# Second feed-forward layer: each quarter of w_ff2 is loaded in the product that first uses it

## The chip, the cores and the metric

The kernel runs on one core of one Trainium2 chip. The metric is the time of one execution in microseconds (us) on the device. Lower is better.

## The reference

One block of a hybrid encoder: 1024 tokens and 16 leading meta tokens of width 1024, everything in float32.

```python
h = h + hybrid_mixer(rmsnorm(h, norm_mix), ...)        # pooling mixer and gated linear attention
h = h + squared_relu_mlp(rmsnorm(h, norm_ffn), w_ff1, w_ff2)
return rmsnorm(h, norm_final)[:, N_META:]

def squared_relu_mlp(u, w_ff1, w_ff2):
    hdn = jnp.square(jax.nn.relu(jnp.einsum('bld,df->blf', u, w_ff1)))   # 1024 -> 4096
    return jnp.einsum('blf,fd->bld', hdn, w_ff2)                         # 4096 -> 1024
```

The change is in the last product, `hdn` by `w_ff2`, and in the loads for it.

## The kernel before

**Arithmetic.** A float32 operand is split in two parts, `hi` (rounded by ScalarE to the matmul's type) and `lo` (the rest, by VectorE); `split` (line 259) issues both, lines 264 and 265. A product is then three matmuls, hi by hi, lo by hi and hi by lo (`mm3`, lines 246 to 248).

**Two layers, in seven products each.** Both feed-forward layers use a Strassen-Winograd scheme: both operands are cut in 2 by 2 quarters, and seven products of sums of quarters take the place of eight. In the first layer, `Quarters.run` makes the hidden values, `ff_result` (line 1490) forms the sums of hidden quarters that the second layer needs, and `keep` stores them in DRAM, one array `hf_dram` for each of the seven (line 1488). There are 16 items (`NPAIR`) of 128 hidden rows in each quarter.

The second layer goes over this table, product by product. A row has the sum of hidden quarters, the sum of quarters of `w_ff2`, and where the result is added (row half, column half, sign):

```python
    FF2 = [
        (S2, "11", ((1, 0, 1), (1, 1, -1))),
        (A22, "21-11", ((0, 0, 1), (1, 0, 1))),
        (S1, "11+22", ((0, 0, 1), (1, 1, 1))),
        (A11, "12-22", ((0, 1, 1), (1, 1, 1))),
        (S6, "11+12", ((1, 1, 1),)),
        (S5, "22", ((0, 0, -1), (0, 1, 1))),
        (S7, "21+22", ((0, 0, 1),)),
    ]
```

So quarter "11" is first used in product 0, "21" in product 1, "22" in product 2 and "12" in product 3.

**One step.** A step is one item `i` of one product `m`. `ff2_raw` (line 1537) issues its loads: `ff2_load` brings the 256 KB of hidden values, called `a` here (the trace names the tile `raw`), into one of four slots, `S["a2"]`; `ff2_weight` brings 256 KB of a quarter of `w_ff2` into its place in `S["w2"]`, where it stays to the end (line 1535). `ff2_operands` (line 1550) forms the sum or difference of two quarters on VectorE, `bt`, in one of two buffers (line 1556), and splits `a` and the weight, each into one of seven slots (`w1h`/`w1l` and `fxh`/`fxl` in the trace). `ff2` (line 1582) then runs 12 matmuls, three into each of four PSUM banks (a bank for each 128 tokens). After the last item of a product the four banks are added to `c` by `add` (lines 1597 and 1599), one addition for each following step.

`c` holds the residual, 8 rows of 512 KB. Row `t` is 128 tokens; rows 0 to 3 are row half 0, rows 4 to 7 row half 1. It is loaded from `h_dram` (line 1547). Products add into rows 4 to 7 after product 0, and into rows 0 to 7 after product 1.

**How far ahead.** `ahead(items, n)` (line 268) runs a generator n items ahead of its user: the loads are issued two items ahead of the operands, the operands two items ahead of the matmuls. A load of `a` has to wait until its slot was split four items before; a split has to wait until TensorE has read the slot it goes to.

**Order.** The order of the instructions on TensorE is that of the program (`manual_schedule`). On the other engines, and on SyncE, which issues all these loads and stores, it is fixed when the program is built, by a scheduler that takes the program's order as its priority and can put an instruction that it holds ready ahead of an earlier one that it doesn't. At run time each engine goes through its order one by one, and one that waits holds up all behind it on its engine.

**Memory.** `ff2_open` (line 1516) lays `w2` and `c` over places of the first layer. "11" lies over operands of the first layer, "21" partly over others that are read to its last product, and `c` over `h`, out of which the last hidden sums are stored. The first load into each has to wait until the last reader of what lay there is done.

In the last product, whose result ends the kernel, the final norm and the stores follow (`finish_row`).

Of the kernel before, what the change touches and what calls it, by code (L numbers as in the profile page):

```python
# [105 lines left out]
def kernel(  # L106
# [1420 lines left out]
    def ff2_load(m, i):  # L1527
        at = S["a2"][(m * NPAIR + i) % len(S["a2"])]
        nc.sync.dma_start(at, hf_of[FF2[m][0]][i])
        return at  # L1530

    def ff2_weight(q, i):
        j, k = int(q[0]) - 1, int(q[1]) - 1
        f = 2 * i + j
        nc.sync.dma_start(S["w2"][q][:, i], w_ff2[f * P : (f + 1) * P, k * HALF : (k + 1) * HALF])

    def ff2_raw():
        for m in range(7):
            for i in range(NPAIR):
                if m == 0:  # L1540
                    ff2_weight("11", i)
                a = ff2_load(m, i)
                if m < 3:
                    ff2_weight(("21", "22", "12")[m], i)
                if m == 0 and i % 2:
                    t = i // 2
                    nc.sync.dma_start(S["c"][:, t], h_dram[t])
                yield m, i, a

    def ff2_operands():  # L1550
        for m, i, a in ahead(ff2_raw(), 2):
            q = FF2[m][1]
            w = S["w2"][q[:2]][:, i]
            if len(q) > 2:
                bt = S["bt"][:, i % 2]
                dve.tensor_tensor(bt, w, S["w2"][q[3:]][:, i], ALU.add if q[2] == "+" else ALU.subtract)  # L1556
                w = bt
            yield m, i, split(a), split(w)
# [140 lines left out]
```

## Time and profile before

| | |
|---|---|
| time, median of 3 | 1243.65 us (1243.61 to 1248.66) |
| the profiled execution's own time | 1241.63 us |
| its span, first to last instruction | 1239.6 us |
| mean granted TensorE clock | 0.996 |
| TensorE matmul busy | 1206.1 us, 97% |
| VectorE busy | 850.9 us, 69% |
| ScalarE busy | 618.8 us, 50% |
| moved by DMA | 173.84 MB, mean 140 GB/s |

Product 0 begins at 923.6 us of the span, and the last matmul starts at 1231.6. The first load into `w2` is issued at 912.2, the last at 1006.7; the eight loads of `c` at 933.2 to 958.6.

In the lines of the profile PE is TensorE's matmul, PEld its weight load, DVE VectorE, ACT ScalarE, and SPq the issuing of DMAs on SyncE. A line of the timeline has the start and duration in us, engine, line and operation, output and inputs, their shapes, and in brackets the idle time of the engine before it and what ended it. A matmul's duration reaches over the start of the next, so the rate is read from the starts.

### The profile page before, as it was taken

Reading aid. Unit: us, or ns where it says so; the run is one execution under the profiler, and the core shown is the slowest. Engines: PE = TensorE matmul, PEld = TensorE weight load, DVE = VectorE, ACT = ScalarE, POOL = GpSimd, SP = SyncE. Lnnn points to the kernel's source line nnn. Section 1 sums busy time; section 2 is a strip of 40 time slices with the busy share of each in tenths; the row PEclk is TensorE's granted clock in tenths of the full one; section 3 lists DMA queues with packets and bytes.
Section 4 is the critical chain, followed back from the end, with each engine's and each line's share of the span. In section 5 each row is a group of like instructions: output and inputs, shape, how many; then the busy total and the mean of one; then the engine's idle time right before and its main releaser. Section 6 shows DMA issues by size and latency. Waiting matters only on the chain.

```text
span 1239.6 us, 18265 instructions
## 1 busy us (share of the span) xinstructions
PE 1206.1 (97%) x6816; PEld 1003.1 (81%) x6816; DVE 850.9 (69%) x1388; ACT 618.8 (50%) x1099; POOL 66.6 (5%) x74
## 2 busy tenths in 40 slices
PE   7999999999999999899999999999999999999997
PEld 6878888988887778688878888888887788888886
DVE  6896676654556676634896676776774877887686
ACT  6667567322446663412654454555553444444554
POOL 2100000001101015400000000000000000000000
PEclk9999999999999999899999999999999999999999
DMA  8033326146102247831244444444569863333432
GB/s 250 2 110 104 110 86 193 53 155 219 36 19 78 69 133 234 282 109 51 98 125 159 156 153 143 162 156 134 176 216 374 289 235 102 94 99 98 162 98 89
DMA packets 142680, 173.84 MB, mean 140 GB/s; under 512 B 10968, under 2 KB 82416, under 8 KB 142592
## 3 DMA queue, kind: packets, MB, share of 16 engines
q1 hardware_dynamic: 142592, 172.68, 43.3%
q8 instruction: 53, 0.87, 0.3%
q14 instruction: 35, 0.29, 0.1%
HBM read 119.17 MB, written 53.48 MB: 139 GB/s over the span
## 4 chain that ended last, share of the span: by engine, by line
PE 85%; DVE 8%; ACT 3%; DMA 2%; issue 2%; SPq 0%; DVEq 0%; ACTq 0%
PE b_mm L246 10%; PE b_mm L247 10%; PE b_mm L248 10%; PE b_ms L247 9%; PE b_ms L246 9%; PE b_ms L248 9%; PE b_x L248 8%; PE b_x L246 8%; PE b_x L247 8%; PE b_sc L1147 1%; PE b_ms L550 1%; PE b_mx L246 1%; PE b_m L1249 1%; PE b_mx L247 1%; PE b_mx L248 1%
## 5 line engine op out<-in xcount | busy, mean ns | idle before, releaser
L246 PE MATMUL b_mm<-th,w1h 128*128 128x512 f32 (+1 forms) x312 | 117.6, 377 | 1.9 <-DVE c L761 1.1
L247 PE MATMUL b_mm<-tl,w1h 128*128 128x512 f32 (+1 forms) x312 | 116.0, 372 | 0.6 <-DVE tl L1407 0.6
L248 PE MATMUL b_mm<-th,w1l 128*128 128x512 f32 (+1 forms) x312 | 115.8, 371 | 0.0
L246 PE MATMUL b_x<-th,w1h 128*128 128x512 f32 (+1 forms) x240 | 90.8, 378 | 0.0
L247 PE MATMUL b_x<-tl,w1h 128*128 128x512 f32 (+1 forms) x240 | 90.6, 378 | 0.0
L248 PE MATMUL b_x<-th,w1l 128*128 128x512 f32 (+1 forms) x240 | 90.3, 376 | 0.0
L264 ACT ACTIVATE w1h<-raw 128x512 fp32r<-128x512 f32 x96 | 59.6, 621 | 36.8 <-PE b_x L247 14.1
L265 DVE TENSOR_TENSOR w1l<-raw,w1h 128x512 fp32r<-128x512 f32 x96 | 65.6, 684 | 12.9 <-ACT w1h L264 12.9
L246 PEld LDWEIGHTS b_mm<-th,w1h 128*128 128x128 f32 x312 | 58.6, 188 | 13.7 <-issue 1.8
L264 ACT ACTIVATE w1h<-fs 128x512 fp32r<-128x512 f32 x72 | 45.4, 631 | 45.8 <-PE b_ms L247 31.5
L247 PEld LDWEIGHTS b_mm<-tl,w1h 128*128 128x128 f32 x312 | 58.6, 188 | 10.6 <-DVE tl L1407 0.9
L248 PEld LDWEIGHTS b_mm<-th,w1l 128*128 128x128 f32 x312 | 58.6, 188 | 10.3
L264 ACT ACTIVATE w1h<-bt 128x512 fp32r<-128x512 f32 x44 | 27.8, 632 | 67.7 <-issue 59.6
L265 DVE TENSOR_TENSOR w1l<-fs,w1h 128x512 fp32r<-128x512 f32 x72 | 49.3, 685 | 14.7 <-ACT w1h L264 14.6
L1556 DVE TENSOR_TENSOR bt<-w,w 128x512 f32<-128x512 f32 x80 | 54.6, 683 | 1.0 <-DMA w<-in_w_ff_dram 1.0
L248 PEld LDWEIGHTS b_x<-th,w1l 128*128 128x128 f32 x240 | 45.1, 188 | 8.4
L246 PEld LDWEIGHTS b_x<-th,w1h 128*128 128x128 f32 x240 | 45.0, 188 | 8.5
L247 PEld LDWEIGHTS b_x<-tl,w1h 128*128 128x128 f32 x240 | 45.1, 188 | 8.3
L264 ACT ACTIVATE fxh<-bt 128x512 fp32r<-128x512 f32 x36 | 22.8, 632 | 55.4 <-issue 48.1
L246 PE MATMUL b_ms<-wo,w1h 128*128 128x512 f32 x128 | 49.8, 389 | 0.0
L247 PE MATMUL b_ms<-wo,w1h 128*128 128x512 f32 x128 | 49.8, 389 | 0.0
L248 PE MATMUL b_ms<-wo,w1l 128*128 128x512 f32 x128 | 49.8, 389 | 0.0
(446 smaller groups left out, 3365.2 us busy)
## 6 DMA issues: line engine op xcount, KB each, us to landing
hf_dram<-h SPq DMA_DIRECT2D x112, 256.0 KB, 2.1
raw<-hf_dram SPq DMA_DIRECT2D x112, 256.0 KB, 2.7
w<-in_w_ff_dram SPq DMA_DIRECT2D x64, 256.0 KB, 4.9
raw<-in_w_in_dram SPq DMA_DIRECT2D x24, 512.0 KB, 4.9
raw<-in_w_ff_dram SPq DMA_DIRECT2D x16, 512.0 KB, 4.1
rawx<-in_w_ff_dram SPq DMA_DIRECT2D x16, 512.0 KB, 4.1
xs<-in_x_dram SPq DMA_DIRECT2D x8, 512.0 KB, 4.7
rawx<-in_w_in_dram SPq DMA_DIRECT2D x8, 512.0 KB, 4.7
```

The costliest lines, as they stand in the source:

```text
L246: pe.matmul(ps, ah, bh, start=first and i == 0, stop=False, skip_group_check=more)
L247: pe.matmul(ps, ah, bl, start=False, stop=False, skip_group_check=more)
L248: pe.matmul(ps, al, bh, start=False, stop=last and i == n - 1, skip_group_check=more)
L264: act.activation(hi, a, ACT.Copy)
L265: dve.tensor_tensor(lo, a, f32(hi), ALU.subtract)
L550: pe.transpose(b[j][:, i], u[:, (4 * j + i) * P : (4 * j + i + 1) * P], ident)
L1147: pe.matmul(b[to, e, j], kk[r, s], qq[r, s], start=True, stop=True, tile_position=(e * CH, u * CH))
L1249: pe.matmul(o[part(u), e, j], scc[part(u), e, j], v[part(u), j, e], start=j == 0, stop=False, tile_position=(u * CH, u * CH), skip_group_c ...
L1556: dve.tensor_tensor(bt, w, S["w2"][q[3:]][:, i], ALU.add if q[2] == "+" else ALU.subtract)
```

## The change

The loads change places in the program, and nothing else. In product 0 only "11" is loaded beside `a`; "21" is loaded in product 1, "22" in product 2, "12" in product 3, each item's weight behind the same item's `a`. Before, "21" came in product 0, "22" in product 1 and "12" in product 2. The rows of `c` came with every second item of product 0, rows 0 to 7 in order; now rows 4 to 7 come with every fourth item of product 0, and rows 0 to 3 with every fourth item of product 1.

```diff
                 if m == 0:
                     ff2_weight("11", i)
                 a = ff2_load(m, i)
-                if m < 3:
-                    ff2_weight(("21", "22", "12")[m], i)
-                if m == 0 and i % 2:
-                    t = i // 2
+                if 0 < m < 4:
+                    ff2_weight(("21", "22", "12")[m - 1], i)
+                if m < 2 and i % 4 == 3:
+                    t = 4 * (1 - m) + i // 4
                     nc.sync.dma_start(S["c"][:, t], h_dram[t])
                 yield m, i, a
```

## The prediction

> **What bounds the kernel now.** I read the page first, then the busy time by stretches, then the matmuls one by one where a stretch isn't full, then the chain of waits back from each gap. On the page (engine busy times, and the chain that ended last by engine):
>
> ```profile
> PE 1206.1 (97%) x6816; PEld 1003.1 (81%) x6816; DVE 850.9 (69%) x1388; ACT 618.8 (50%) x1099; POOL 66.6 (5%) x74
> PE 85%; DVE 8%; ACT 3%; DMA 2%; issue 2%; SPq 0%; DVEq 0%; ACTq 0%
> ```
>
> TensorE bounds it, and the change leaves every matmul as it is. So it can win only what TensorE idles in the second layer, and lose only by new idling there. The stretches of that layer (product 0 with the start of product 1; the rest of product 1; the rest; columns: length, busy time and count by engine, clock, DMA share, GB/s):
>
> ```profile
> 923.00:971.00 48.00, 45.78 (x199) 36.45 (x197) 26.61 (x44) 19.27 (x33) 0.00 (x0) 1.00 0.98 354
> 971.00:1015.00 44.00, 44.00 (x195) 36.42 (x195) 36.22 (x59) 19.75 (x36) 0.00 (x0) 1.00 0.84 277
> 1015.00:1226.00 211.00, 211.00 (x933) 174.74 (x932) 164.63 (x279) 96.45 (x178) 0.00 (x0) 1.00 0.34 102
> ```
>
> Only the first has idle time, 2.22 us, at a DMA share of 0.98; from 971 on TensorE is full. The matmuls around the gaps (start, duration, line, tiles):
>
> ```profile
> 939.73 0.39 PE L248 MATMUL b_ms<-fxh,w1l 128*128 128x512 f32 x1
> 941.25 0.50 PE L246 MATMUL b_x<-fxh 128*128 128x512 f32 x1 [1.14 <-ACT fxh L264]
> ...
> 942.55 0.39 PE L247 MATMUL b_x<-fxl,fxh 128*128 128x512 f32 x1
> ...
> 960.70 0.39 PE L246 MATMUL b_x<-fxh 128*128 128x512 f32 x1
> ...
> 963.19 0.39 PE L248 MATMUL b_ms<-fxh,fxl 128*128 128x512 f32 x1
> 964.59 0.50 PE L246 MATMUL b_x<-w1h 128*128 128x512 f32 x1 [1.01 <-ACT w1h L264]
> ...
> 965.97 0.40 PE L247 MATMUL b_x<-w1l,w1h 128*128 128x512 f32 x1
> ```
>
> From 960.70 to 963.19 twelve matmuls start, so one takes 2.49/11 = 0.226 us, and a step of 12 takes 2.72 us. The first gap: 939.73 to 942.55 is 5 starts, 2.82 us instead of 1.13, so 1.69 us are lost with the slow restart behind it. The second: 963.19 to 965.97 is 5 starts, 2.78 instead of 1.13, so 1.65 us. Together 3.3 us, 0.27% of the kernel. This is the most the change can take from the profiled run.
>
> **Where the two gaps come from.** The first, by the chain of waits in order of time:
>
> ```profile
> 928.45 4.65 DMA hf_dram<-h
> 933.23 0.33 SPq L1547
> 933.60 0.43 SPq L1547
> 934.08 1.40 SPq L1547
> 935.52 5.02 DMA raw<-hf_dram
> 940.57 0.64 ACT fxh L264
> ```
>
> The sync queue held the first three loads of `c` (line 1547). `c` lies where `h` lay, so the first of them waited until the last store out of `h` had landed at 933.1. Behind them stood the load of item 6 of product 0 (935.52), which then took 5.02 us. Its slot in `a2` had been free since VectorE ended the split of item 2 at 923.6, 11.9 us earlier:
>
> ```profile
> 922.93 0.68 DVE L265 TENSOR_TENSOR fxl<-raw,fxh 128x512 fp32r<-128x512 f32 x1
> ```
>
> The second gap is one of order on ScalarE:
>
> ```profile
> 960.70 0.63 ACT L264 ACTIVATE w1h<-w 128x512 fp32r<-128x512 f32 x1 [2.08 <-DMA w<-in_w_ff_dram]
> 963.39 0.63 ACT L264 ACTIVATE fxh<-bt 128x512 fp32r<-128x512 f32 x1 [2.06 <-PE b_ms L247]
> 963.92 0.61 ACT L264 ACTIVATE w1h<-raw 128x512 fp32r<-128x512 f32 x1
> ```
>
> At 963.39 ScalarE split `bt`, which only product 1 needs, and had waited for a slot that TensorE gave back. Behind it in its fixed order stood the split of the `raw` that product 0 needed next (963.92), and TensorE waited for that one. `bt` could be so early because the quarter "21" was already there in product 0.
>
> **What the change removes and moves.** Sizes and landings, the last line from a stretch where the loads of `a` are alone and the line before it from 940 to 970:
>
> ```profile
> w<-in_w_ff_dram SPq DMA_DIRECT2D x64, 256.0 KB, 4.9
> c<-h_dram SPq DMA_DIRECT2D x8, 512.0 KB, 6.6
> ...
> raw<-hf_dram SPq DMA_DIRECT2D x11, 256.0 KB, 6.0
> ...
> raw<-hf_dram SPq DMA_DIRECT2D x34, 256.0 KB, 2.7
> ```
>
> No load is added or dropped: 64 of `w2`, 8 of `c`, 112 of `a`. In program order product 0 now asks for 48 loads of 256 KB and 8 of 512 KB, 16.8 MB in 16 x 2.72 = 43.5 us, 386 GB/s. After the change it asks for 32 and 4, 10.5 MB, 241 GB/s. Product 1 goes from 8.4 MB (193 GB/s) to 10.5 (241), product 2 stays at 193, product 3 goes from 4.2 MB (96) to 8.4 (193). All of these lie under the 354 GB/s that the first stretch moved. The cost in bytes is nil, and the peak is cut by over a third.
>
> *First gap.* Item 6 now comes in the program behind one load of `c` (with item 3) instead of three, and behind no load of "21". The sync queue before it:
>
> ```profile
> 912.23 2.33 SPq L1535 DMA_DIRECT2D w<-in_w_ff_dram  x5
> ...
> 918.36 1.88 SPq L1535 DMA_DIRECT2D w<-in_w_ff_dram  x4
> ...
> 925.25 1.63 SPq L1535 DMA_DIRECT2D w<-in_w_ff_dram  x3
> ...
> 928.83 1.84 SPq L1535 DMA_DIRECT2D w<-in_w_ff_dram  x3
> ...
> 1005.73 1.38 SPq L1535 DMA_DIRECT2D w<-in_w_ff_dram  x3
> ```
>
> If the `c` load still stands ahead of it and waits until 933.1, item 6 issues two loads of `c` earlier, 935.52 - 0.43 - 1.40 = 933.7, and lands between 2.7 and 6.0 us later, 936.4 to 939.7. With the split of 0.64 TensorE could start at 937.0 to 940.4, where it needs it at 939.73 + 0.23 = 939.96. The loss is 0 to 0.4 us plus its slow restart, instead of 1.69. If it goes ahead of `c`, the loss is nil. I take nil, since the load beside it falls.
>
> *Second gap.* "21" now comes behind all of "11", so the first `bt` of product 1 is ready later, and items 14 and 15 land sooner. The split of `raw` should come first. Bounds 0 to 1.65 us of gain; I take 1.65, because both things that made the wrong order are weakened.
>
> *What is late next: the weights of products 1 to 3.* Each load now stands right behind the `a` load of its own item, and that waits for a slot. The `a` load of item 0 of product 3 (the 49th) and the `bt` of the same item (the 33rd), when all runs smoothly:
>
> ```profile
> 1040.72 0.32 SPq L1529 DMA_DIRECT2D raw<-hf_dram  x1
> ...
> 1048.77 0.68 DVE L1556 TENSOR_TENSOR bt<-w,w 128x512 f32<-128x512 f32 x1
> ...
> DMA to landing us min/median/max: 3.0/4.9/7.2
> ```
>
> A weight issued behind that load, at 1041.05, has 1048.77 - 1041.05 = 7.7 us until VectorE wants it. The third line is the landing of all 64 weight loads, in the crowded stretch: median 4.9, worst 7.2. So even strictly just in time it is hidden, by 0.5 us at worst. If that cover went, VectorE would wait at `bt`, with the two `lo` subtractions and the additions into `c` queued behind it, and TensorE behind those. It may not come to that: at 1005.73 the last weight of product 2 is issued while TensorE is still in product 1, so the queue runs ahead of the program when `a` loads wait for slots. Rows 0 to 3 of `c` are used first after product 1, rows 4 to 7 after product 0: each comes with the product before. Cost 0.
>
> Sum: 3.3 us off. The profiled run took 1241.63 us for a span of 1239.6 (2.03 outside), so 1238.3 for that run. It was 2.02 us under the median of 1243.65; the same 3.3 us off the median give **1240.4 us**, 0.27% less. A measurement of this kernel can tell about 0.5%, 6.2 us, from no change, so this counts as the same.
>
> **The rivals.**
>
> *No gain.* The fixed orders come out with new gaps in place of the old, or the queue runs ahead into "21" and keeps the DMA engines as full in product 0 as now. For it: the queue does run ahead, and no byte is dropped. Against it: what runs ahead comes behind what is needed. Time 1243.7.
>
> *More than the profile shows.* The three times of before reach from 1243.61 to 1248.66, and the profiled run lies 2.0 us under their median. If the difference is further waiting in the crowded first stretch, 3.3 + 2.0 to 3.3 + 7.0 us go: 1233.4 to 1238.4. It counts as faster under 1237.4. Against it: a spread of that size can come from anywhere.
>
> *Order on ScalarE, slower.* With a weight coming close to its use, the order fixed at build can put the split of a later item ahead of the one that TensorE needs, as at 963.39, in any of the 48 steps of products 1 to 3. Each costs 1.65 us. Six make up the gain and the 6.2 us ((6.2 + 3.3)/1.65 = 5.8); at one step in six, 8 of them, it is 13.2 - 3.3 = +9.9, 1253.6. For it: the profile shows one such step just where loads and `bt` meet. Against it: products 1 and 2 already make `bt` of weights that came recently, and show no gap after 971.
>
> *Weights late, slower.* Place: `bt` of products 1 to 3. From the slot's release (1040.68) to that `bt` are 8.1 us, three steps, so a wait comes back every third step, 16 times. If the worst landing (7.2) meets a queue held up as before 933 (from 928.83 + 1.84 to 933.23, 2.6 us), it is 9.8 - 7.7 = 2.1 us, 16 x 2.1 = 34 us: 1243.7 + 34 - 3.3 = 1274. It counts from 0.6 us ((6.2 + 3.3)/16), a landing of 8.3 us in every cycle. No landing in the table is that long. [...]
>
> **How the numbers follow.** The forecast 0.42; no gain 0.24; more than the profile shows, beyond 0.5%, 0.14; order 0.14; late weights 0.06. So faster 0.14, same 0.66, slower 0.20. The range goes from 1237, the edge of the third case, to 1254, which takes in the order rival at its price; late weights and the rest of the third case are left out, up to about 0.2. Within the likeliest sign alone it would be 1238 to 1246.
>
> **What would show it.** Right: TensorE busy over all of 923 to 971; item 6 of product 0 loaded before 934.5; the landing of `a` in 940 to 970 clearly under 6.0 us; no row of `bt` waiting for DMA in products 1 to 3; the rest of the span alike. Wrong: VectorE waiting for DMA at line 1556; ScalarE splitting `bt` right after a wait while TensorE idles; idle TensorE after 971, where there is none now; or the gap of 1.7 us still there behind the first load of `c`.

## The result and the profile after

The changed kernel took 1237.99 us (median of 6 runs, 1237.36 to 1239.98), the kernel before beside it 1245.8 us: a ratio of 0.9942, 95% interval 0.9928 to 0.9955, or 7.2 us less (5.6 to 9.0). In a second comparison, on one chip together with the first four runs below, it was 1239.16 to 1244.68 us, 0.9958 (0.9943 to 0.9972), 5.2 us less (3.5 to 7.1). The forecast was 3.3 us less, 1240.4 us, in a range from 1237 to 1254. The kernel is faster beyond the noise, and by more than forecast. Over the 0.5% at which the prediction speaks of faster it is not clearly: both intervals hold 0.5%.

The stretches of the second layer after the change (columns as in the prediction):

```profile
923.00:971.00 48.00, 48.00 (x214) 39.76 (x213) 31.01 (x50) 22.81 (x40) 0.00 (x0) 1.00 0.94 328
971.00:1015.00 44.00, 44.00 (x196) 36.47 (x195) 35.31 (x57) 18.46 (x32) 0.00 (x0) 1.00 0.95 327
1015.00:1226.00 211.00, 211.00 (x933) 174.81 (x932) 163.93 (x277) 96.80 (x179) 0.00 (x0) 1.00 0.36 102
```

TensorE's 45.78 us of 48 became 48.00: both gaps are gone. But the DMA engines are as full as before (0.94 and 0.95 of the time, where it was 0.98 and 0.84), and the first stretch still moves 328 GB/s where the forecast had 241 asked for. The sync queue shows why (timeline of SyncE after the change):

```profile
927.40 0.62 SPq L1529 DMA_DIRECT2D raw<-hf_dram  x1
...
935.80 0.79 SPq L1547 DMA_DIRECT2D c<-h_dram  x2
936.69 0.38 SPq L1529 DMA_DIRECT2D raw<-hf_dram  x1
...
963.49 1.38 SPq L1535 DMA_DIRECT2D w<-in_w_ff_dram  x3
```

The load of item 6, at 935.52 before, is now issued at 927.40, ahead of the first load of `c`, and waits for nobody. Where the loads of `a` wait for slots the queue runs ahead into the next quarters, up to three loads between two of `a`. ScalarE at the end of product 0, where a split of `bt` stood ahead of the last two splits of `raw`:

```profile
958.96 0.61 ACT L264 ACTIVATE w1h<-raw 128x512 fp32r<-128x512 f32 x1
961.14 0.63 ACT L264 ACTIVATE w1h<-w 128x512 fp32r<-128x512 f32 x1 [1.56 <-PE b_ms L247]
961.67 0.62 ACT L264 ACTIVATE fxh<-raw 128x512 fp32r<-128x512 f32 x1
963.86 0.63 ACT L264 ACTIVATE fxh<-bt 128x512 fp32r<-128x512 f32 x1 [1.57 <-PE b_ms L247]
```

Now the splits that product 0 needs come first, and `bt` behind them. The whole layer is best measured from the start of its first matmul to the start of its last (TensorE's timeline after the change):

```profile
925.80 0.39 PE L246 MATMUL b_x<-w1h 128*128 128x512 f32 x1
...
1230.22 0.39 PE L248 MATMUL b_ms<-fxh,fxl 128*128 128x512 f32 x1
```

That is 304.4 us. Before it was from 923.6 to 1231.6, 308.0. The profiled spans differ by only 1239.6 - 1238.2 = 1.4 us, because the layer began 2.2 us later in the profile after; where that comes from is told at the end. Below, "the layer" is this length, and its value in each profile stands in one table:

| kernel | layer, us | ratio to before, 95% interval |
|---|---|---|
| before, six profiles | 308.0, 308.4, 310.6, 308.9, 308.4, 310.7; mean 309.2 | 1.0007 (0.9998 to 1.0016) for the copy b_again |
| after, two profiles | 304.4, 304.4 | 0.9942 (0.9928 to 0.9955); 0.9958 (0.9943 to 0.9972) |
| w_only | 304.4 | 0.9953 (0.9941 to 0.9966) |
| c_only | 304.8 | 0.9962 (0.9950 to 0.9975) |
| c_second_half | 308.1 | 0.9990 (0.9980 to 0.9999) |
| c_first_half | 312.7 | 1.0022 (1.0012 to 1.0033) |
| jit | 304.4 | 0.9959 (0.9943 to 0.9975) |

### The profile page after: what moved, and what is told of

It reads as the page before. It is cut to its first block, busy times and chain, and to the rows that moved or that the text cites. A ratio compares the mean times of both kernels' runs of the same rounds, so it can differ in the third digit from the quotient of the medians.

```text
span 1238.2 us, 18288 instructions
## 1 busy us (share of the span) xinstructions
PE 1207.4 (98%) x6816; PEld 1006.6 (81%) x6816; DVE 852.3 (69%) x1388; ACT 618.3 (50%) x1099; POOL 66.3 (5%) x74
## 4 chain that ended last, share of the span: by engine, by line
PE 87%; DVE 7%; ACT 3%; issue 1%; DMA 1%; SPq 0%; DVEq 0%; ACTq 0%
PE b_mm L246 10%; PE b_mm L247 10%; PE b_mm L248 10%; PE b_ms L248 9%; PE b_ms L246 9%; PE b_ms L247 9%; PE b_x L247 8%; PE b_x L246 8%; PE b_x L248 8%; PE b_sc L1147 1%; PE b_ms L550 1%; PE b_mx L246 1%; PE b_m L1249 1%; PE b_mx L248 1%; PE b_mx L247 1%
```

## The experiments

Two questions were open. Was it the order, as forecast, or the mere number of bytes asked for in product 0? And why did the clock on the wall save more than the 3.5 us that the first two profiles show?

### The kernel before, and the change, once more

No edit in either.

> The kernel before, unchanged, to see how far its two gaps vary. Three explanations are open for the measured 7 us where the profiles show 3.5. Theory A, varying gaps: the two gaps end on DMAs, so they differ from run to run, and the profiled run had short ones; a second profile shows a total over 3.5 us, up to 7. Theory B, two gaps of fixed size, and the rest is drift between chips or sessions: again 3.5 us in total to within 0.5. By both the ratio to the kernel before is 1.000 within 0.001.

> The changed kernel, unchanged, on the same chip as the kernel before. Theory A: ratio 0.994, as first measured, 7 us. Theory B: 0.997, the 3.5 us of the two gaps. Either way no gap over 0.3 us in the second layer.

The copy of before agrees with before to 0.0007, so a comparison on one chip can be off by about 0.001. Its layer took 308.4 us, 4.0 above the changed kernel. The changed kernel gave 0.9958, between the two theories; its interval holds 0.997 and ends just short of 0.994. This decided nothing yet.

### Half of the change each

For w_only, the kernel before with the weights' part of the diff alone:

```diff
-                if m < 3:
-                    ff2_weight(("21", "22", "12")[m], i)
+                if 0 < m < 4:
+                    ff2_weight(("21", "22", "12")[m - 1], i)
```

> The weights moved as in the change, the eight loads of c left in product 0 as before. Order theory (the queue's and ScalarE's fixed order made the gaps): the loads of items 6 to 9 of product 0 now stand ahead of the first load of c, and the split of bt stands behind the last splits of product 0, so both gaps are gone and the ratio is that of the whole change, within 0.001. Crowd theory (the bytes asked for in product 0 made the gaps): 4.2 of the 6.3 MB that the change takes out of product 0 are taken out here, so two thirds of the gain, 0.996 where the whole change has 0.994, and a gap of about 1 us is left.

For c_only, the other part alone:

```diff
-                if m == 0 and i % 2:
-                    t = i // 2
+                if m < 2 and i % 4 == 3:
+                    t = 4 * (1 - m) + i // 4
```

> The rows of c moved as in the change, the weights left as before. Order theory: the split of bt comes behind the last splits of product 0, so the second gap of 1.65 us is gone; one load of c in place of three stands ahead of item 6, so the first gap goes from 1.7 us to 0 to 0.4 plus its slow restart. At least 2.6 of the 3.5 us are saved. Crowd theory: 2.1 of 6.3 MB leave product 0, so a third of the gain, about 1.2 us of the 3.5, and both gaps are still there.

Each half does nearly all of it alone: no gap in w_only, 0.3 us in c_only. By bytes they should have left a third and two thirds of the loss. In w_only TensorE's first stretch is full while eight loads of `c` are still in it (52 us from 925):

```profile
925.00:977.00 52.00, 52.00 (x231) 43.09 (x230) 35.32 (x58) 24.18 (x42) 0.00 (x0) 1.00 0.94 332
```

c_only tells more. Its quarter "21" is loaded in product 0 as before, and yet the split of `bt` comes behind the last split that product 0 needs (ScalarE in c_only, the last `raw` of product 0 and the first `bt`):

```profile
963.37 0.63 ACT L264 ACTIVATE w1h<-raw 128x512 fp32r<-128x512 f32 x1
...
964.87 0.63 ACT L264 ACTIVATE fxh<-bt 128x512 fp32r<-128x512 f32 x1 [0.87 <-PE b_ms L247]
```

So the early "21" alone doesn't make the second gap. It goes when the weights move (w_only), and as well when the loads of `c` move (c_only).

For the first gap, one load of `c` still stands ahead of item 6 in c_only and waits for `h` (SyncE, then ScalarE):

```profile
936.05 0.33 SPq L1547 DMA_DIRECT2D c<-h_dram  x1
936.42 0.43 SPq L1529 DMA_DIRECT2D raw<-hf_dram  x1
...
941.01 0.63 ACT L264 ACTIVATE fxh<-raw 128x512 fp32r<-128x512 f32 x1 [3.07 <-DMA raw<-hf_dram]
```

It is issued 10.0 us after product 0 began (926.5). In b_again it was issued at nearly the same point, 10.1 us after the start, but behind three loads of `c`. The chain of waits of b_again:

```profile
935.27 0.33 SPq L1547
...
936.11 0.43 SPq L1547
...
936.59 7.20 DMA raw<-hf_dram
...
943.80 0.64 ACT fxh L264
```

4.6 us to land in the one, 7.2 in the other. One pair doesn't fix the price, though: over the six profiles of before the load of item 6 took 4.9 to 8.0 us to land, and the least where the queue had been slowest to issue the three loads ahead (3.0 us; 1.3 us where it took 8.0). The sum varies less. From the issue of the first load of `c` to the landing of item 6 it is 4.9 us behind one load, 7.3 to 9.4 us (mean 8.2) behind three, and 12.1 us behind six in c_first_half below. So each load of 512 KB ahead of it delays this small urgent load by about 1.4 us, an estimate from the one and the six, (12.1 - 4.9)/5. Part of it is in the queue, which took 4.16 us to issue the six, and part in the landing, 4.6 us behind one and 7.85 behind six.

### The same bytes, in another order

Two more places for the eight loads of `c`, with everything else as before. Here the bytes of product 0 don't change.

```diff
-                if m == 0 and i % 2:
-                    t = i // 2
+                if m == 0 and i < 8:      # c_first_half
+                    t = i
```

> The kernel before with the eight loads of c in items 0 to 7 of product 0: the same bytes in every product, but six loads of c, not three, stand ahead of the load of item 6 and wait with it until h is free; the split of bt now stands behind the last splits of product 0. Order theory: the first gap grows by three loads of 512 KB, each 0.4 to 1.4 us by the times that the queue took for them, so by 1.3 to 4.2 us to 3 to 6 us, and the second gap is gone; the layer takes 307 to 310.5 us from the first matmul to the last, where it took 308.0 to 308.4 before and 304.4 after the change. Crowd theory: the bytes are the same, so both gaps stay as they are, 308.0 to 308.4.

```diff
-                if m == 0 and i % 2:
-                    t = i // 2
+                if m == 0 and i >= 8:     # c_second_half
+                    t = i - 8
```

> The kernel before with the eight loads of c in items 8 to 15 of product 0: the same bytes in every product, but the loads of items 6, 7 and 8 stand ahead of the first load of c; on ScalarE two splits of bt, not one, now stand ahead of splits that product 0 needs. Order theory: the first gap is gone, the second stays or doubles: 1.65 to 3.3 us, the layer takes 306 to 307.7 us. Crowd theory: the same bytes, so both gaps stay, 308.0 to 308.4, the first at the same step.

The bytes theory falls. With six loads of `c` ahead the first gap alone is 6.4 us of idle time, and the second is gone (c_first_half: SyncE, the landing in the chain of waits, then TensorE):

```profile
934.52 4.16 SPq L1547 DMA_DIRECT2D c<-h_dram  x6
938.73 0.44 SPq L1529 DMA_DIRECT2D raw<-hf_dram  x1
```

```profile
938.73 7.85 DMA raw<-hf_dram
```

```profile
940.54 0.39 PE L248 MATMUL b_ms<-fxh,w1l 128*128 128x512 f32 x1
947.28 0.80 PE L246 MATMUL b_x<-fxh 128*128 128x512 f32 x1 [6.36 <-ACT fxh L264]
```

The gap is larger than the 3 to 6 us expected, and behind it TensorE's granted clock was 0.50 from 947.2 to 950.6, by an estimate 3.4 x 0.5 = 1.7 us more; together they make up the 8.2 us by which this layer is longer than 304.4. The kernel is slower than before (1.0022). With the loads of `c` behind items 6 to 8 the first gap is gone, and the second comes twice, because two splits of `bt` now stand ahead of others (ScalarE in c_second_half; each time TensorE waited for the split of `raw` in the second line of the pair):

```profile
963.31 0.63 ACT L264 ACTIVATE fxh<-bt 128x512 fp32r<-128x512 f32 x1 [2.65 <-PE b_ms L247]
963.84 0.61 ACT L264 ACTIVATE w1h<-raw 128x512 fp32r<-128x512 f32 x1
...
967.69 0.63 ACT L264 ACTIVATE w1h<-bt 128x512 fp32r<-128x512 f32 x1 [2.72 <-PE b_ms L247]
968.23 0.61 ACT L264 ACTIVATE w1h<-raw 128x512 fp32r<-128x512 f32 x1
```

The layer is 308.1 us, 3.7 over the 304.4 without gaps and 0.4 over the range expected. Each of the two splits costs what it was priced at: from 963.11 to 965.89 and from 967.49 to 970.27 five matmuls start, 2.78 us in place of 1.13, so 1.65 us are lost each time. The other 0.4 us are a hitch close behind, where a weight load of TensorE waits for a `lo` of VectorE:

```profile
972.78 0.19 PEld L248 LDWEIGHTS b_ms<-fxh,fxl 128*128 128x128 f32 x1 [0.49 <-DVE fxl L265]
```

The total happens to lie where the bytes theory had it, but the gaps are all at the end of product 0 and none is at item 6, where that theory had one.

### Weights just in time

```diff
                 a = ff2_load(m, i)
+                recent.append(a)
                 if 0 < m < 4:
-                    ff2_weight(("21", "22", "12")[m - 1], i)
+                    q = ("21", "22", "12")[m - 1]
+                    pool.tensor_copy(S["w2"][q][:, i, 0:1], recent[-3][:, 0:1])
+                    ff2_weight(q, i)
```

> The changed kernel with each weight of products 1 to 3 forced to come just in time: GpSimd writes one column of the weight's place, out of the a tile of two items before, ahead of the load, so the queue can't run ahead by more than two items. The output is unchanged. By the reckoning of the prediction (7.7 us from issue to use, 3.0 to 7.2 us to land) nothing is late: the layer takes 304.4 us within 0.5, the last weight is issued in product 2 or 3 and not in product 1, the ratio is that of the changed kernel, 0.995 within 0.0015. By the rival of late weights each third step waits 0.6 us or more: 16 such waits, 10 us or more, slower than the kernel before.

The changed kernel doesn't itself test whether late weights are harmless, as its queue runs ahead. This one does (the weight loads in jit: all of them, then the landing of the 44 issued after 960; and the stretches):

```profile
L1535 SPq DMA_DIRECT2D w<-in_w_ff_dram x64: 332/333/736, 912.9 to 1084.8; - x64
...
  DVE bt L1561: 3.6, 4
...
DMA to landing us min/median/max: 2.5/3.4/6.1
...
DMA to landing us min/median/max: 2.5/3.0/4.2
```

```profile
977.00:1015.00 38.00, 38.00 (x170) 31.45 (x169) 28.84 (x47) 16.13 (x28) 3.73 (x12) 1.00 0.58 188
1015.00:1224.00 209.00, 209.00 (x924) 173.01 (x923) 162.65 (x275) 96.93 (x177) 9.23 (x26) 1.00 0.44 136
```

The last weight is now issued at 1084.8, where it was 1010.3 with the change alone. VectorE waited for weights four times, 3.6 us in all, and TensorE never: 38.00 of 38 and 209.00 of 209. Item by item the weights of products 1 to 3 are issued 2.8 to 9.1 us ahead of the `bt` that needs them (median 5.3); with the change alone it was 4.1 to 77.9 us (median 41). So this is tighter than the 7.7 us of the prediction. But the weights also land sooner there, in 3.0 us in the median and in no more than 4.2, with the DMA engines busy for 0.58 and 0.44 of the time. The ratio is that of the changed kernel.

### The kernel before, three to six

No edit.

> A third profile of the kernel before. Theory A, varying gaps: a total over 4.5 us in the second layer. Theory B, gaps of fixed size: 3.5 to 4.0 us, as in the first two.

> A fourth profile of the kernel before. Clock theory: the length of the first gap varies with the landing of the load of item 6, and where TensorE idles about 2 us there, its granted clock goes to 0.5 for 3.4 us, which costs about 1.7 us more. So a profile has a first gap either under 2 us of idle time with the clock at 1.0, 308.0 to 308.5 us for the layer, or over 2 us with a stretch at 0.5, 310 us or more. Constant theory: 308.0 to 308.5 with the clock at 1.0 in all three of this call, the third profile was an exception.

> A fifth profile, as the fourth. If half of the six profiles have the stretch at 0.5, the mean loss in the layer is about 5 us, which is within the intervals of the measured gain of the change (5.2 and 7.2 us).

> A sixth profile of the kernel before, with the same expectations as the fourth and the fifth: 308.0 to 308.5 us for the layer without a stretch at clock 0.5 in it, 310 us or more with one.

The third profile's layer took 310.6 us, and its stretches around the first gap show another cost behind the gap itself (the clock is the last column but two):

```profile
941.70:944.00 2.30, 0.23 (x2) 0.00 (x0) 0.00 (x0) 0.62 (x2) 0.00 (x0) 1.00 0.99 330
...
945.10:948.50 3.40, 3.40 (x10) 2.59 (x9) 0.93 (x2) 0.82 (x2) 0.00 (x0) 0.51 1.03 398
948.50:949.00 0.50, 0.50 (x4) 0.41 (x3) 0.43 (x1) 0.04 (x1) 0.00 (x0) 0.93 1.05 393
```

After the gap TensorE's granted clock fell to half for 3.4 us, in which matmuls start every 0.43 us, not 0.23. Of the six profiles, the four without that have a layer of 308.0 to 308.9, the two with it 310.6 and 310.7. The first gap varies in all of them. It was 1.14 us of idle time in the profile that the prediction shows; the first matmul behind it in b_again, b_5, b_4, b_third and b_6, the idle time in brackets:

```profile
944.49 0.50 PE L246 MATMUL b_x<-fxh 128*128 128x512 f32 x1 [1.54 <-ACT fxh L264]
```

```profile
943.81 0.50 PE L246 MATMUL b_x<-fxh 128*128 128x512 f32 x1 [1.61 <-ACT fxh L264]
```

```profile
944.05 0.50 PE L246 MATMUL b_x<-fxh 128*128 128x512 f32 x1 [2.08 <-ACT fxh L264]
```

```profile
944.06 0.50 PE L246 MATMUL b_x<-fxh 128*128 128x512 f32 x1 [2.13 <-ACT fxh L264]
```

```profile
944.36 0.80 PE L246 MATMUL b_x<-fxh 128*128 128x512 f32 x1 [2.68 <-ACT fxh L264]
```

From 1.14 to 2.68 us, and the profile that the prediction was made from has the shortest of the six. So "varying gaps" holds, and the half clock of the clock theory too, but the clock theory's condition, a gap of over 2 us, does not: b_4's gap of 2.08 us brought no drop, and its layer lies 0.4 us above the 308.5 expected without one. What went with a drop and what did not is in the last section. Gaps of fixed size fall. The mean loss is 309.2 - 304.4 = 4.8 us. Set against it, the ratios, each to the kernel before on the same chip, say 5.2 (after), 5.9 (w_only, to a layer shorter by 4.8), 4.7 (c_only, 4.4), 5.1 (jit, 4.7), 1.2 (c_second_half, 1.0), and 2.7 slower (c_first_half, 3.5). The layer accounts for all six within their intervals. The 7.2 us of the first comparison lie further off: its interval ends at 5.6. That comparison was made with other runs of before, and what the rest of it is stays open. Apart from before and after, each layer is from a single profile.

## Why the prediction was right, and where it was short

**Right: what bounds it, and the two causes.** The gain came from TensorE's idle time in the first stretch and nowhere else. The load of item 6 went ahead of `c`, and the split of `bt` behind those of product 0. The profile's layer fell by 3.56 us, the forecast of 3.3 and a last small hitch of 0.2 near 971. The reason given for the second gap was half of it: c_only and c_first_half load "21" in product 0 as before, and the gap is gone there as well. With more loads of `c` at the end of product 0 (c_second_half) it comes twice. So the loads around items 14 and 15, the second thing that the prediction named, are enough to make or remove it; whether the later "21" alone would do, no run separates, since moving "21" takes loads away from there too.

**Right: late weights are hidden.** TensorE waited for no weight, even with the running ahead taken away. The rival of late weights falls by jit. The reckoning behind it, 7.7 us from issue to use against a worst landing of 7.2, is not what was tested: in jit a weight had 5.3 us in the median, and landed in at most 4.2. Where the cover went, VectorE did wait at `bt`, four times and 3.6 us in all, but TensorE not behind it. The order rival, slower, didn't occur: TensorE has no gap in products 1 to 3. Its price was right, 1.65 us for each in c_second_half.

**Short: the first gap.** The term that was mis-sized is the 1.69 us of the first gap. It was read from one profile, where the idle part was 1.14 us; in five more it was 1.54 to 2.68, in two of them with the half clock behind it, which the sum did not have. The load of item 6 took up to 8.0 us to land there, and 5.02 in the profile that was read. With 4.8 us for both gaps in place of 3.3 the forecast would have been 0.39% less, and the second comparison gave 0.42%. So it was in part the rival "more than the profile shows", and by the mechanism it guessed, waiting in the crowded first stretch; it had 0.14, for a gain over 0.5%. Whether the gain is over 0.5% the two comparisons leave open: 0.58% and 0.42%, with 0.5% in both intervals.

**Luck: the place in the range.** 1237.99 us lies 1 us above the lower edge. The forecast counted down from the 1243.65 us of three executions; beside the changed kernel, before took 1245.8. The ratio of 0.9942 taken from 1243.65 would be 1236.4 us, outside the range.

**Wrong in detail: the peak of the DMA.** "The peak is cut by over a third" counted what each product asks for in program order. The queue ran ahead, as the same part had thought possible, and the engines were as full as before. That this cost nothing, and that the bytes of before cost 3.7 us in one order and 8.2 in another, shows that the peak was not the term that mattered. Nor was "no row of `bt` waiting for DMA" right: VectorE waited twice after the change, 1.1 us in all, without TensorE idling.

## What to carry to other kernels

The order of the sync queue was a resource of its own here: the load of item 6 was issued at 935.52 behind three loads of `c`, the first of which waited for `h`, and at 927.40 ahead of them. So a load that must wait for memory to come free, and a large one that nobody needs soon, belong behind the small ones that are needed next. Here the DMA engines were busy for 0.98 of the first stretch with the gaps and 0.94 without them. An idle gap that ends on a DMA should be priced from several profiles: this one went from 1.14 to 2.68 us over six, and in two of them the clock was at half behind it for 3.41 us. The weights could be moved late because their landing, measured where they then come, stayed mostly under the time to their use (in jit 3.0 us against 5.3 in the median, with four waits of VectorE, 3.6 us in all, and none of TensorE); this was worth doing not for the bytes but for what then stands ahead of what.

## What the runs showed of the hardware

TensorE's granted clock fell to half behind idle times of 2.13 us (b_third), 2.68 (b_6) and 6.36 us (c_first_half) in this layer, and not behind 2.08 us (b_4) or less. Two gaps as close as 2.08 and 2.13 us differ in it, so the length alone does not tell them apart. Within a trace the changes of the clock lie at distances that are whole multiples of 3.41 us: the slow stretches behind the three gaps last 3.41, 3.41 and 6.83 us, and in the profile before the changes at 519.23, 526.06 and 1236.03 are 6.83 and 709.97 us apart, 2 and 208 times 3.413. So each trace can be counted off from its changes in windows of 3.41 us. The gap of b_third lies within one window, in which TensorE is busy for 1.28 us. That of b_4 is cut by a border at 942.73, 121 windows behind the change of the clock at 529.72, and TensorE is busy for 2.65 and 2.09 us in the two windows (b_third, then b_4; columns as in the prediction):

```profile
941.75:945.16 3.41, 1.28 (x5) 0.63 (x5) 1.12 (x2) 1.61 (x3) 0.00 (x0) 1.00 0.99 348
945.16:948.57 3.41, 3.41 (x10) 2.63 (x9) 0.87 (x2) 0.80 (x2) 0.00 (x0) 0.50 1.04 400
```

```profile
939.32:942.73 3.41, 2.65 (x12) 1.87 (x10) 0.69 (x1) 0.37 (x1) 0.00 (x0) 1.00 0.86 311
942.73:946.14 3.41, 2.09 (x8) 1.43 (x9) 1.99 (x3) 1.78 (x3) 0.00 (x0) 1.00 1.03 402
```

Counted through the 13 traces in this way, from 20 to 1230 us of the span, every window at full clock in which TensorE, by its busy time in the trace, was idle for 52% or more was followed by one at half clock, and none with 50% or less was. So the gap of 2.13 us came with half the clock and a layer of 310.6 us (b_third), and that of 2.08 us with the full clock and 308.9 (b_4). The window ahead of a drop was not idle throughout: TensorE is busy for 1.28 of the 3.41 us in that of b_third. Nor do the windows begin at the same point of the two runs: the gaps lie at 941.93 to 944.06 and at 941.97 to 944.05, and the border nearest to the start of each at 941.75 (b_third) and 942.73 (b_4). All this is a count over these traces; why the clock changes, they do not show.

The 2.2 us by which the layer began later in the profile after come from far ahead of the change. The same matmul starts 1.2 us later than in the profile before at 20 us of the span already. Most of the rest, 1.1 us, comes between 517 and 530 us, where TensorE idles and runs at half clock for a while, by amounts that vary (0.50 from 519.23 to 526.06 before, from 521.79 to 528.62 after; the stretch before, then after):

```profile
522.00:540.00 18.00, 16.96 (x69) 13.91 (x69) 10.07 (x11) 5.54 (x7) 0.00 (x0) 0.89 0.86 282
```

```profile
522.00:540.00 18.00, 15.53 (x59) 12.41 (x60) 10.01 (x11) 7.91 (x9) 1.27 (x1) 0.82 0.86 295
```

In all the profiles here the layer began between 923.6 and 926.8 us, whichever kernel it was. A span of one profile is therefore no measure of a change of a few us; the length of the stage is.
